# Roll along rows: half rows of two neighbours per DMA in place of one whole row

## The chip, the cores and the metric

The kernel runs on one core of one Trainium2 chip. The metric is the device time of one execution in microseconds. Data moves through 16 DMA engines that serve several queues; the queues that matter here are filled by SyncE (SP), ScalarE (ACT) and GpSimd (POOL).

## The reference

```python
def reference(x, shift):              # x: 8192 x 8192 float32, shift = 100
    return np.roll(x, shift, axis=1)
```

Every row is moved right by 100 elements (400 bytes), and its last 100 elements become its first. There is no arithmetic: 268.44 MB are read and 268.44 MB written.

## The kernel before

Each row of 8192 elements (32 KB) is cut at column `a` of the output. With `s = 100`, line 20 gives 128 and line 22 raises it to `a = 256`; `g = a - s = 156`.

**Bodies.** Columns `a` to 8192 of the output (7936 elements, 31744 bytes a row) are copied straight from HBM to HBM, from columns 156 to 8092 of the input. The rows are seen as 128 blocks of 64, and a block as 16 groups `e` of four neighbouring rows `j` (lines 34 and 35). One DMA at line 44 takes row `j` of each of the 16 groups: the trace gives it 16 pieces of 31744 bytes. Its 16 rows stand four rows (128 KB) apart, one for each DMA engine, so an engine gets four neighbouring rows one after another from four DMAs. SP starts at block 0 and goes up, with `j` rising; ACT starts at block 127 and goes down, with `j` falling (line 42). The two loops run in step for `i` from 0 to 63. For the last two values of `i` each row is issued as two DMAs of one half each, cut at `mid = 4224`: `parts` in line 40.

No body depends on another. On each of the two queues the semaphores that the framework gives out turn in fours, so from the fifth DMA on an issue waits until the DMA four before it has landed.

**Heads.** Columns 0 to 255 of the output go through on-chip tiles on GpSimd's queue: 16 tiles of 512 rows, four rows to each of 128 partitions. Line 73 loads, in runs of 1024 bytes, the last 100 elements of one row together with the first 156 of the next, for three of the four rows; lines 74 and 77 load what is missing at the ends; VectorE puts the pieces into place (lines 75 and 78), and line 81 writes 256 columns of all 512 rows. All tiles have buffers of their own.

Of the kernel before, what the change touches and what calls it, by code (L numbers as in the profile page):

```python
# [1 line left out]

# [4 lines left out]


@with_exitstack
def kernel(  # L10
    ctx: ExitStack,
    tc: tile.TileContext,
    x: bass.AP,
    shift: int,
    out: bass.AP,
):
    nc = tc.nc
    n_rows, n_cols = x.shape
    s = shift % n_cols
    a = -(-s // 128) * 128  # L20
    if 0 < a <= 384 and a + 128 <= n_cols:
        a += 128
    g = a - s
    P = nc.NUM_PARTITIONS
    engines = [nc.sync, nc.scalar]
    n_chunks = 16
    rows = n_rows // n_chunks

    xm = x.rearrange("(c e j) w -> c j e w", e=16, j=4)
    om = out.rearrange("(c e j) w -> c j e w", e=16, j=4)
    if a < n_cols:
        blocks = n_rows // 64
        mid = (a + n_cols) // 256 * 128
        for i in range(blocks // 2):
            parts = ((a, mid), (mid, n_cols)) if i >= blocks // 2 - 2 and a < mid else ((a, n_cols),)  # L40
            for j in range(4):
                for eng, c, q in ((engines[0], i, j), (engines[1], blocks - 1 - i, 3 - j)):
                    for lo, hi in parts:
                        eng.dma_start(out=om[c, q, :, lo:hi], in_=xm[c, q, :, lo - s:hi - s])
    if a == 0:
        return


    if a > 512:
        for i in range(n_chunks):  # L50
            r = slice(i * rows, (i + 1) * rows)
            nc.gpsimd.dma_start(out=out[r, :s], in_=x[r, n_cols - s:])
            if g > 0:
                nc.gpsimd.dma_start(out=out[r, s:a], in_=x[r, :g])
        return

    Q = 4
    n_st = n_rows // (P * Q)
    reads = ctx.enter_context(tc.tile_pool(name="reads", bufs=n_st))
    heads = ctx.enter_context(tc.tile_pool(name="heads", bufs=n_st))
    xt = x.rearrange("(k p q) c -> k p q c", q=Q, p=P)
    ot = out.rearrange("(k p q) c -> k p q c", q=Q, p=P)
    tiles = []
    for k in range(n_st):
        t = reads.tile([P, Q - 1, a], x.dtype)
        h = heads.tile([P, Q, a], x.dtype)  # L70
        lead = bass.AP(tensor=x.tensor, offset=(k * P * Q + 1) * n_cols - s,
                       ap=[[Q * n_cols, P], [n_cols, Q - 1], [1, a]])
        nc.gpsimd.dma_start(out=t[:], in_=lead, single_packet=True)  # L73
        nc.gpsimd.dma_start(out=h[:, Q - 1, :s], in_=xt[k, :, Q - 1, n_cols - s:], single_packet=True)  # L74
        nc.vector.tensor_copy(h[:, :Q - 1, :s], t[:, :, :s])  # L75
        if g > 0:
            nc.gpsimd.dma_start(out=h[:, 0, s:], in_=xt[k, :, 0, :g], single_packet=True)  # L77
            nc.vector.tensor_copy(h[:, 1:, s:], t[:, :, s:])  # L78
        tiles.append(h)
    for k, h in enumerate(tiles):  # L80
        nc.gpsimd.dma_start(out=ot[k, :, :, :a], in_=h[:], single_packet=True)  # L81


# [1 line left out]
_INS = ['x', 'shift']  # L85
_OUTS = [((8192, 8192), 'float32')]

_NUMBERS = {'shift': 100}


# [26 lines left out]
```

## Time and profile before

| what | value |
|---|---|
| median of 3 runs | 816.4 us (815.55 to 817.09) |
| the profiled execution | 817.74 us, of which 816.0 us is the span of the profile |
| GpSimd busy | 41.3 us in 68 instructions |
| VectorE busy | 12.0 us in 32 instructions |
| issues of whole-row DMAs | 248 on SP, 248 on ACT, 496 KB each |
| issues of half-row DMAs (the last two `i`) | 16 on SP, 16 on ACT, 248 KB each |
| issues for the heads | 64 on GpSimd's queue |

The span runs from the first to the last recorded work; the profiled execution's own time contains it. "DMA" rows give the busy share of the 16 DMA engines in tenths for 40 equal slices, and GB/s what they moved (each byte once, though an HBM to HBM copy both reads and writes it). In the list of queues, q1 is SP's, q10 is ACT's and q0 is GpSimd's; the columns are packets, MB, and the time that the packets took as a share of 16 engines' span. The packet records hold queue, size, start and duration of each packet, but not the number of its engine. In the list of DMA issues the columns are KB of each and median us from issue to landing.

### The profile page before, as it was taken

The page shows a single profiled execution, that of the slowest core. Times are in us where ns is not written, and L with a number is a line of the kernel's source. Part 1 is how long each engine was busy: PE and PEld are TensorE (multiplying, and loading weights), DVE is VectorE, ACT ScalarE, POOL GpSimd, SP SyncE. Part 2 cuts the span into 40 slices and gives each one's busy share as a digit, 9 for nine tenths or more (in the row PEclk, how much of TensorE's full clock was granted, in tenths as well). Part 3 has the DMA queues.
Part 4 walks back from the last instruction along what each step waited for, and adds up shares of the span by engine and source line. Part 5 has one row for each costly group of instructions (what it writes and reads, how often), then busy time and mean ns, then how long its engine had stood idle before and what let it go on. Part 6 is the DMA issues. An engine that isn't in the chain of part 4 may idle for free. (4 is left out here: it accounts for less than half of the span.)

```text
span 816.0 us, 689 instructions
## 1 busy us (share of the span) xinstructions
DVE 12.0 (1%) x32; POOL 41.3 (5%) x68
## 2 busy tenths in 40 slices
DVE  0000000000000000000000000000000000000000
POOL 2001011101110110000000000000000000000000
DMA  9999999999999999999999999999999999999998
GB/s 315 348 338 362 340 353 342 355 336 347 338 355 348 350 365 354 353 352 347 352 355 344 328 336 324 335 333 336 333 332 336 333 327 341 328 332 333 339 302 297
DMA packets 22277, 276.90 MB, mean 339 GB/s; under 512 B 9472, under 2 KB 9728, under 8 KB 13824
## 3 DMA queue, kind: packets, MB, share of 16 engines
q1 hardware_dynamic: 8448, 130.04, 46.6%
q10 hardware_dynamic: 8448, 130.04, 43.7%
q0 software_dynamic: 5376, 16.78, 8.6%
q14 instruction: 5, 0.04, 0.0%
HBM read 268.44 MB, written 268.44 MB: 658 GB/s over the span
## 5 line engine op out<-in xcount | busy, mean ns | idle before, releaser
L81 POOL DMA_DIRECT2D out_dram<-h x16 | 11.4, 715 | 146.7 <-DMA out_dram<-h 91.7
L77 POOL DMA_DIRECT2D h<-in_x_dram x16 | 8.7, 542 | 156.0 <-DMA t<-in_x_dram 156.0
L73 POOL DMA_DIRECT2D t<-in_x_dram x16 | 12.2, 762 | 23.6 <-DMA h<-in_x_dram 22.8
L74 POOL DMA_DIRECT2D h<-in_x_dram x16 | 8.9, 559 | 37.2 <-DMA h<-in_x_dram 37.2
L75 DVE COPY h<-t 128x300 f32<-128x300 f32 x16 | 5.9, 367 | 271.5 <-DMA t<-in_x_dram 271.5
L78 DVE COPY h<-t 128x468 f32<-128x468 f32 x16 | 7.5, 468 | 0.0
L98 POOL MEMSET const-float32-0.0<- 128x1 f32 x1 | 0.1, 99 | 0.2 <-issue 0.2
L98 POOL MEMSET const-bfloat16-1.0<- 128x1 bf16 x1 | 0.1, 102 | 0.0
L98 POOL MEMSET const-float32-1.0<- 128x1 f32 x1 | 0.1, 99 | 0.0
L98 POOL MEMSET const-uint8-127<- 128x1 uint8 x1 | 0.1, 99 | 0.0
## 6 DMA issues: line engine op xcount, KB each, us to landing
out_dram<-in_x_dram SPq DMA_DIRECT2D x248, 496.0 KB, 12.7
out_dram<-in_x_dram ACTq DMA_DIRECT2D x248, 496.0 KB, 12.7
out_dram<-h POOLq DMA_DIRECT2D x16, 512.0 KB, 105.6
t<-in_x_dram POOLq DMA_DIRECT2D x16, 384.0 KB, 47.8
out_dram<-in_x_dram SPq DMA_DIRECT2D x16, 248.0 KB, 6.0
out_dram<-in_x_dram ACTq DMA_DIRECT2D x16, 248.0 KB, 5.9
h<-in_x_dram POOLq DMA_DIRECT2D x16, 78.0 KB, 41.6
h<-in_x_dram POOLq DMA_DIRECT2D x16, 50.0 KB, 47.5
```

What stands on the lines that cost most here:

```text
L73: nc.gpsimd.dma_start(out=t[:], in_=lead, single_packet=True)
L74: nc.gpsimd.dma_start(out=h[:, Q - 1, :s], in_=xt[k, :, Q - 1, n_cols - s:], single_packet=True)
L75: nc.vector.tensor_copy(h[:, :Q - 1, :s], t[:, :, :s])
L77: nc.gpsimd.dma_start(out=h[:, 0, s:], in_=xt[k, :, 0, :g], single_packet=True)
L78: nc.vector.tensor_copy(h[:, 1:, s:], t[:, :, s:])
L81: nc.gpsimd.dma_start(out=ot[k, :, :, :a], in_=h[:], single_packet=True)
L98: nc = _bacc.Bacc("TRN2", target_bir_lowering=False, num_devices=1)
```

## The change

For `i` from 0 to 61 the four DMAs of a block are cut the other way. Where a DMA took row `j` whole for each of the 16 groups, it now takes one half (columns 256 to 4223, or 4224 to 8191, 15872 bytes each) of two neighbouring rows of each group. The order on SP in a block is: left halves of rows 0 and 1, right halves of rows 0 and 1, left halves of rows 2 and 3, right halves of rows 2 and 3. ACT takes rows 2 and 3 first and then 0 and 1, also left halves before right. The `rearrange` puts `e` outermost, so the 16 groups still go to the 16 engines. Bytes and issues stay as they were. The last two values of `i` and the heads are untouched.

```diff
         for i in range(blocks // 2):
             parts = ((a, mid), (mid, n_cols)) if i >= blocks // 2 - 2 and a < mid else ((a, n_cols),)
+            if len(parts) == 1 and a < mid:
+                for j in (0, 2):
+                    for lo, hi in ((a, mid), (mid, n_cols)):
+                        for eng, c, q in ((engines[0], i, j), (engines[1], blocks - 1 - i, 2 - j)):
+                            eng.dma_start(out=om[c, q:q + 2, :, lo:hi].rearrange("j e w -> e j w"),
+                                          in_=xm[c, q:q + 2, :, lo - s:hi - s].rearrange("j e w -> e j w"))
+                continue
             for j in range(4):
                 for eng, c, q in ((engines[0], i, j), (engines[1], blocks - 1 - i, 3 - j)):
                     for lo, hi in parts:
```

## The prediction

> **What bounds the kernel now.** I read the DMA rows first, because sections 1 and 5 of the page hold only 12.0 us of VectorE and 41.3 us of GpSimd work in a span of 816.0 us. From the page:
>
> ```profile
> DMA  9999999999999999999999999999999999999998
> DMA packets 22277, 276.90 MB, mean 339 GB/s; under 512 B 9472, under 2 KB 9728, under 8 KB 13824
> q1 hardware_dynamic: 8448, 130.04, 46.6%
> q10 hardware_dynamic: 8448, 130.04, 43.7%
> q0 software_dynamic: 5376, 16.78, 8.6%
> HBM read 268.44 MB, written 268.44 MB: 658 GB/s over the span
> ```
>
> The 16 DMA engines are busy from end to end: 46.6 + 43.7 + 8.6 = 98.9%. q1 (SP) and q10 (ACT) carry the row bodies, HBM to HBM; q0 (GpSimd) carries 16.78 MB of row heads through the on-chip tiles. Busy is not full speed, though. In the packet records, 31744 B (one row body) takes 1173 ns at best, 1430 ns on average (1475 on q1, 1384 on q10); only a third are under 1185 ns. So engines mostly hold a packet longer than they need to move it. What holds them shows in the same window view, first with GpSimd's queue running and then with the copies alone:
>
> ```profile
> 20.00:490.00 470.00, 11.94 (x32) 35.95 (x56) 1.00 1.00 347
> 490.00:760.00 270.00, 0.00 (x0) 0.00 (x0) 1.00 0.99 333
> ```
>
> The last column is GB/s moved, the one before it the DMA share. A copied byte is both read from and written to HBM; a GpSimd byte touches HBM once. The DMA view of the first stretch has 16.23 MB on q0, 34.5 GB/s over 470 us. HBM traffic is therefore 2 x 347 - 34.5 = 659.5 GB/s in the first and 2 x 333 = 666 in the second: two mixtures that differ by 14 GB/s in bytes moved agree within 1% in HBM traffic. I read the bound as the memory's throughput under this pattern, about 660 GB/s, and not the number of packets.
>
> Then the issuers, in the waits of SP's queue and the DMA issues:
>
> ```profile
> SPq L44 <- DMA out_dram<-in_x_dram: 670.1, 258, 5.1
> out_dram<-in_x_dram SPq DMA_DIRECT2D x248, 496.0 KB, 12.7
> out_dram<-in_x_dram SPq DMA_DIRECT2D x16, 248.0 KB, 6.0
> ```
>
> SP sits waiting 670.1 us: the trace's semaphores on this queue turn in fours, so an issue waits for the DMA four before it. Four DMAs in flight on each queue, 12.7 us from issue to landing, is a full backlog; issue time (510 ns on SP, 517 on ACT) is off the path.
>
> **The change, part by part.** Per block of 64 rows each queue still issues four DMAs of 496 KB in place of four of 496 KB, for all but the last two values of i. So the 248 + 248 whole-row DMAs, their semaphores, their waits and their bytes stay; each of the 16 engines now gets two pieces of 15872 B where it got one of 31744 B.
>
> Packets: 496 DMAs x 16 engines = 7936 pieces become 15872, 496 more per engine. Undisturbed, the trace has 1175 ns (median of the quick ones) for a whole row and 592 ns (median on q1 and q10) for a half, which the last 32 DMAs already carry: 2 x 592 - 1175 = 9 ns per split, 496 x 9 ns = 4.5 us if every one showed. Two thirds of the packets are held longer than they need anyway and hide it; a third run at full speed. I take 4.5 / 3 = 1.5 us, with 0 (all covered by memory stalls) and 4.5 us (none covered) as ends.
>
> The Trainium skill, page "DMA: Bandwidth & Descriptors", section "How a descriptor splits into AXI transactions", says a descriptor that doesn't start on a multiple of 256 B reads from the boundary below it and discards what lies before. The new right halves start in the source at byte 4124 x 4 = 16496, 112 past such a boundary, so by that page (an estimate) 7936 x 112 B = 0.9 MB more would be read, 1.3 us at 660 GB/s; no row of this trace can show it.
>
> Order: an engine takes one packet from q1, then one from q10 (chained by end and start, 1401 of the 1712 row packets of q10 between 420 and 750 us follow a q1 row directly). With half pieces I expect the turns to come at half rows, so four address streams (two reads, two writes) alternate twice as often, and each 32 KB row is visited in two visits with its neighbour's half between. Traffic under finer mixing is what this trace shows least. The nearest rows are the two stretches: with GpSimd's pieces of 400 to 4096 B in the turn, traffic is 1% lower (659.5 against 666), which over the kernel would be 8 us. On the other side stands the best 20 us slice of the copy-only part, 341 GB/s against 333, worth 2.3% or 19 us less if it held throughout; the worst there is 322 to 324, 3% or 25 us more. The last 32 DMAs say that half rows by themselves are harmless: mean packet 708 ns against 1430 / 2 = 715, landing 6.0 against 12.7 / 2 = 6.35 us, though those run as the backlog drains. I take 2 us, a quarter of the 8: pieces of 15872 B are far longer than GpSimd's.
>
> Completion: an SP DMA now ends after ACT's first half too, about one half piece (0.7 us) later in its turn. That shifts SP's next issue once and is hidden by three more DMAs queued behind; if that cover were gone, engines would idle, where they now have a share of 0.99. What SP and ACT queue behind the wait is only more copies, so nobody else is late.
>
> GpSimd: its packets stand in the same turns. If turns halve, its loads land sooner (now 47.8 us for 384 KB) and its last issue comes well before 404 us. That moves when its 16.78 MB go, not how many bytes the memory carries: cost 0. The drain after 780 us keeps its DMAs unchanged.
>
> Sum: 1.5 + 2 = 3.5 us. On the profiled execution (817.74 us, of which 816.0 is span) that is 821.2; the median of the runs is 816.4, 1.3 below that execution, so 820 us.
>
> **The rivals.** *Hidden altogether* (816.4, within 0.2%): the splits vanish in memory stalls and order makes no difference; the steady 660 GB/s speaks for it. The change may also not interleave at all: if an engine takes both pieces of a DMA in one turn, only the 9 ns splits are left, at most 4.5 us.
>
> *Faster*: the pattern, not the bytes, sets the 660 GB/s. Whole-row turns let one stream hold an engine for up to 3.3 us (longest row packet); shorter turns even out the engines and spread the accesses. Place: the copies throughout; price: half of the way from 333 to 341 GB/s, 1.2% or 10 us, 806 us. It decides once the copy-only stretch rises above about 335 GB/s. For it: the spread of packet times, and a rate that wanders from 322 to 341 with nothing else changed. Against it: two different mixtures reach the same traffic, as a ceiling would have it.
>
> *Much slower*: the 16 engines work on rows 128 KB apart (four rows of 32 KB), now all in the same half of their rows for a whole DMA; if that crowds fewer parts of memory, the rate falls to the worst slices, 323 GB/s, 3%: 841 us. Against it: whole rows also start together and keep 333 to 347. [...]
>
> **How the numbers follow.** A measurement of this kernel can tell about 0.2% (1.6 us) from no change. Forecast, a small loss of 818 to 824 us: 0.38. Much slower, 824 to 845: 0.17. Hidden: 0.14. Faster: 0.31, most of it between 803 and 814. So slower 0.55, same 0.14, faster 0.31. The range 803 to 836 leaves out the last fifth of the way from 816.4 to the 841 of the worst slices and the gains beyond 1.6%, about one case in ten. Both signs hold much of the chance; the forecast's own range is 818 to 824.
>
> **What would show it.** Unchanged: 248 + 248 issues of 496 KB, DMA share 9 throughout, 510 ns issues. Packets rise by 7936 to about 30200. The copy-only stretch should fall from 333 to about 331 or 332 GB/s, and section 3 should show q1 and q10 a little busier for the same 130.04 MB. If turns halve, GpSimd's loads land clearly below 47.8 us and its last L81 issue comes before 404 us. I am wrong if the copy-only rate is at 335 or above (memory liked the order) or below 325 (it disliked it), or if engine share falls under 0.97 (issue became the bound).

## The result: 819.1 against 816.8 us, and the profile after

The changed kernel takes 819.08 us (median of 15 runs), the kernel before 816.81 us (15 runs beside it): ratio 1.0027, 95% interval 1.0018 to 1.0035, so 2.3 us slower (1.5 to 2.9). The profiled execution takes 819.45 us, 817.7 of it span. Its page, with the rows in the order shown of before:

```profile
DMA  8999999999999999999999999999999999999998
DMA packets 30213, 276.90 MB, mean 339 GB/s; under 512 B 9472, under 2 KB 9728, under 8 KB 13824
q1 hardware_dynamic: 12416, 130.04, 47.1%
q10 hardware_dynamic: 12416, 130.04, 43.9%
q0 software_dynamic: 5376, 16.78, 8.0%
HBM read 268.44 MB, written 268.44 MB: 657 GB/s over the span
```

7936 packets more (30213 - 22277), the same bytes, engines still busy throughout, and 657 in place of 658 GB/s of HBM traffic. Against before, q1 is up 0.5 and q10 0.2 points of engine time and q0 is down 0.6. The same stretches as before:

```profile
20.00:490.00 470.00, 11.27 (x30) 34.57 (x54) 1.00 1.00 348
490.00:760.00 270.00, 0.00 (x0) 0.00 (x0) 1.00 0.99 332
```

The copies alone run at 332 GB/s where they ran at 333: 0.3% as rounded, 0.2% by the packet records (663.3 against 664.7 GB/s of HBM traffic). The 348 against 347 of the first stretch is no gain: GpSimd's packets are now gone by 378 us (507 us before), and the copies that fill the rest of the stretch move fewer bytes a second; the HBM traffic of that stretch is 660.4 GB/s in both. Summed over the packet records, the new kernel's HBM traffic is behind by 0.7 us at 20 us, 0.8 at 350, 1.6 at 440, 0.5 at 500, 1.3 at 750 and 1.7 at 805 (bytes missing at 663 GB/s). The gap wanders by about 1 us, so one pair of profiles can't tell where in the run the 1.7 us between the two spans are lost. The issues:

```profile
SPq L45 <- DMA out_dram<-in_x_dram: 636.4, 244, 5.0
out_dram<-in_x_dram SPq DMA_DIRECT2D x248, 496.0 KB, 12.6
t<-in_x_dram POOLq DMA_DIRECT2D x16, 384.0 KB, 37.4
L45 SPq DMA_DIRECT2D out_dram<-in_x_dram x248: 571/571/717, 0.7 to 782.8; - x124
```

The last line (durations in ns, least/median/most, then the first and last start in us) shows an issue at 571 ns where a whole row's took 510; with 636 us of waiting in front of them the issues hide that. GpSimd's loads land in 37.4 in place of 47.8 us, and its last write is issued at 298 us in place of 404.

### The profile page after: what moved, and what is told of

Same layout as the page of the kernel before. It is cut to its first block, busy times and chain, and to the rows that moved or that the text cites. A ratio compares the mean times of both kernels' runs of the same rounds, so it can differ in the third digit from the quotient of the medians.

```text
span 817.7 us, 689 instructions
## 1 busy us (share of the span) xinstructions
DVE 12.0 (1%) x32; POOL 41.2 (5%) x68
## 2 busy tenths in 40 slices
DMA packets 30213, 276.90 MB, mean 339 GB/s; under 512 B 9472, under 2 KB 9728, under 8 KB 13824
## 5 line engine op out<-in xcount | busy, mean ns | idle before, releaser
L80 POOL DMA_DIRECT2D t<-in_x_dram x16 | 12.2, 760 | 13.6 <-DMA h<-in_x_dram 12.7
## 6 DMA issues: line engine op xcount, KB each, us to landing
t<-in_x_dram POOLq DMA_DIRECT2D x16, 384.0 KB, 37.4
```

## The experiments

They ran in three later jobs, each on another chip, where the kernel before took 826.9, 829.9 and 829.1 us, so ratios to it are compared; where two profiles of different jobs are set side by side, the text says so. The first job held the change once more, the half pieces in old order, the crossed pairs and the quarters; the third held the eighths, with and without heads and at both shifts, and the two rows per DMA; the second held the rest. In the code, "..." and comments stand for lines left out, and a line with "-" is what the new one takes the place of; the last two values of `i` stay as they were.

**Theories.** *Split*: the loss is the number of pieces, a fixed cost for each. *Order*: it is the row left half way. My prediction had both, 1.5 and 2 us. A rival for the cause is that finer turns let GpSimd's small packets in more often.

**The change once more**, to compare with the other kernels of the first of these jobs:

> The change itself, beside the others on one chip: 1.0027 within 1.0018 to 1.0035.

Measured: 1.0027 (1.0016 to 1.0038).

**Half pieces, old order.** Each engine walks its rows from start to end as before, but a DMA carries the right half of one row and the left half of the next:

```diff
-eng.dma_start(out=om[c, q, :, a:n_cols], in_=xm[c, q, :, a - s:n_cols - s])
+...                                    # half DMAs at the two ends of each queue
+row = (c * 64 + q) * n_cols
+# nxt: next row of this engine on this queue (j + 1, or the next block's first)
+ap = [[4 * n_cols, 16], [nxt + a - row - mid, 2], [1, mid - a]]
+eng.dma_start(out=bass.AP(tensor=out.tensor, offset=row + mid, ap=ap),
+              in_=bass.AP(tensor=x.tensor, offset=row + mid - s, ap=ap))
```

> Half-row pieces in the order of before: a DMA carries the right half of one row and the left half of the next, so each engine walks its rows from start to end as before, but in pieces of 15872 B with two per DMA (one extra half DMA at each end of each queue). Theory 1, the split: the loss comes from the number of pieces (9 ns each, partly covered) and from turns at half rows, so this kernel loses the same, ratio to before about 1.003 (819 us). Theory 2, the order: the loss comes from leaving a row half way and coming back to it, so this kernel is at 1.000 (817 us). Both at once, as predicted (1.5 us for the split, 2 us for the order): 1.001 to 1.002. If the pieces stand in finer turns, GpSimd's loads land in about 37 us as after the change, in every theory.

Measured: 1.0024 (1.0012 to 1.0037). That is the change's loss without the change's order. What is left for the order is 0.03%, some 0.2 us, with about 1.4 us either way. GpSimd's loads land in 35.1 us, near the 37 expected, so turns are finer here too. One side effect: a DMA that runs from the end of one row to the start of the next has the head columns between its two pieces, and the framework makes the heads' writes wait for bodies. The waits of this kernel show it; before, the longest wait of that line was for earlier writes of heads, 91.7 us in total:

```profile
POOL out_dram L96 <- DMA out_dram<-in_x_dram: 612.0, 15, 91.2
```

The heads' writes are spread over the whole run there (the last q0 packet ends at 810 us), and yet the time is that of the changed kernel. So where the heads' bytes fall in time seems to cost nothing, unless it happens to offset the order; no run has one without the other.

**Crossed pairs.** A DMA carries the left half of one row and the right half of its neighbour, the next DMA the two others (set against the changed kernel):

```diff
-    for lo, hi in ((a, mid), (mid, n_cols)):
+    for first, step in ((a, n_cols + w), (mid, n_cols - w)):      # w = mid - a
...
+            ap = [[4 * n_cols, 16], [step, 2], [1, w]]
```

> The same pieces and DMAs as after the change, other pairs: a DMA carries the left half of one row and the right half of the next, the following DMA the two halves left over. Theory 1 (the split): as after the change, 1.003. Theory 2 (the order): the row is left half way as often as after the change, so also about 1.003, but if it matters whether the pieces of a DMA lie in the same half of the row (all engines in one half, the rival of crowding), it falls back to 1.000 to 1.001.

Measured: 1.010 (1.0062 to 1.0139), and this takes in only the three quickest of its six runs (830.6, 836.7 and 839.1 us); the others took 863.4 to 897.3, and the profiled one is the longest, with a span of 895.5. It does not answer its question, since the pattern brought waits of its own: the instructions rise from 689 to 937, 244 of the 248 more are semaphore instructions of SP and ACT, and SP's longest wait grows from 5.1 to 9.4 us. The framework evidently takes DMAs to overlap that share no element. Here and in the half pieces of the old order the two pieces of a DMA lie in different rows and in different columns of them; the change and the eighths, whose DMAs take the same columns of every row and span each other's columns as well, have the 689 instructions of before. From 200 to 760 us:

```profile
200.00:760.00 560.00, 0.00 (x0) 7.15 (x10) 1.00 0.88 301
```

Engine share 0.88 and 301 GB/s: here engines run out of work. It is a picture of the case that the prediction named as its third alarm (share under 0.97), by waits and not by issue time, and the change itself avoids it.

**More splits.** Quarters of four rows per DMA, then eighths (each DMA: two eighths of four rows), bytes and number of DMAs kept:

```diff
-parts = ((a, mid), (mid, n_cols)) ... else ((a, n_cols),)          # before: whole rows
+for lo in range(a, n_cols, w):                                     # w = (n_cols - a) // 4
+    for eng, c in ((engines[0], i), (engines[1], blocks - 1 - i)):
+        eng.dma_start(out=om[c, :, :, lo:lo + w].rearrange("j e w -> e j w"),
+                      in_=xm[c, :, :, lo - s:lo - s + w].rearrange("j e w -> e j w"))
```
```diff
+ap = [[4 * n_cols, 16], [n_cols, 4], [4 * w, 2], [1, w]]           # w = (n_cols - a) // 8
+for lo in range(a, mid, w): ...
```

Quarters:

> The change carried one step on: a DMA carries one quarter (7936 B) of four neighbouring rows per engine, so 23808 splits in place of 7936 and turns at quarter rows. Theory 1 (the split): three times the splits, so three times the loss, about 1.008 (823 us); with the stalls covering a rising share, at least 1.005. Theory 2 (the order): each row is visited four times in place of two, three returns in place of one: also up to 1.008, but as the pieces shrink it may fall either way. A ceiling of the memory that nothing of this touches: 1.003 again. GpSimd's loads should land sooner still, about 30 us, if turns are taken at each piece.

Eighths:

> Eighth pieces (3968 B): a DMA carries the eighths n and n + 4 of four neighbouring rows per engine, 55552 splits, same bytes and number of DMAs. With 4.6 ns of an engine per split, as halves and quarters gave: 16 us, ratio 1.019. If the heads' packets are what finer turns disturb, the loss flattens (the heads can't get sooner than at full turns): 1.012.

Measured: quarters 1.0084 (1.0066 to 1.0102), eighths 1.0190 (1.0165 to 1.0214). GpSimd's loads land in 24.6 us with quarters and 14.9 with eighths. With 7936, 23808 and 55552 splits the losses are 0.27, 0.84 and 1.90%: 0.27 to 0.28% for each 7936 splits. That is a straight line through nothing, as a fixed price would have it: 15.8 us over 3472 splits per engine is 4.5 ns for one, halves (2.2 us over 496) give 4.5 and quarters 4.7. But the line alone doesn't prove a fixed price, since more than the number of splits differs: all halves and quarters start 112 B past a multiple of 256 B in the source, while every second eighth starts 240 B past one there and 128 B past one in the output (3968 is 15.5 times 256); and whether order costs anything was tried for halves only. The loss shows in the copy-only stretch of the eighths, where the half rows had 328 GB/s in the first of these jobs. q1 and q10 together hold 93.7% of the engines' time, 91.3% there, but part of that is time that GpSimd's queue no longer holds (5.9 in place of 8.2%):

```profile
490.00:760.00 270.00, 0.00 (x0) 0.00 (x0) 1.00 1.00 319
q1 hardware_dynamic: 36224, 130.04, 49.7%
q10 hardware_dynamic: 36224, 130.04, 44.0%
```

**Without heads.** Columns 0 to 255 are not written:

```diff
-    if a == 0:
+    if a > 0:
         return
```

> The kernel before without the heads (columns 0 to 255 of the output are not written). A ceiling of the memory at about 660 GB/s: 16.78 MB of 536.9 MB less HBM traffic, 3.1% less time, ratio 0.969. A bound by the DMA engines' own time: the share of GpSimd's queue, 8.6%, falls away, ratio 0.914.

> Quarter pieces without the heads (columns 0 to 255 are not written), to set beside the bodies of before without heads. If a split costs about 4.5 ns of an engine wherever it stands, this is 0.8% above that kernel. If the loss came from GpSimd's packets getting more turns, the two are the same within 0.2%.

> Eighth pieces without the heads (columns 0 to 255 are not written), against the bodies of before without heads, 0.9656. Cost of a split independent of the heads: the same 16 us, 0.985. Quarters lost 0.34% without heads and 0.84% with them; if that holds on, 7/3 of 0.34% here: 0.8%, ratio 0.973.

Measured: before without heads 0.9656 (0.9644 to 0.9669). That is near the 0.969 of a ceiling on HBM traffic and far from the 0.914 of a bound by engine time. The window from 20 to 760 us of that kernel, then of the quarters and of the eighths without heads:

```profile
20.00:760.00 740.00, 0.00 (x0) 1.00 1.00 327
```
```profile
20.00:760.00 740.00, 0.00 (x0) 1.00 1.00 325
```
```profile
20.00:760.00 740.00, 0.00 (x0) 1.00 1.00 323
```

Engine share stays at 1.00 with a queue's 8.6% gone: the copies' packets are held longer (31744 B now 1538 ns on average over both queues). Busy engines here are waiting engines. By the packet records this kernel moves 655 GB/s of HBM traffic from 20 to 760 us; in the same job whole rows with heads, at a shift of 128, move 654. So reads and writes of HBM together are what is level; whether the memory itself or the way to it sets that level, no run here tells. Quarters are at 0.9689 and eighths at 0.9821, so against the bodies alone the loss is 0.34% (about 0.18 either way) and 1.71% (0.22, across two jobs). Eighths lose nearly what they lost with heads (1.90%), so most of the price of a split is the bodies' own. Quarters lose less than half of their 0.84% in time, though the two profiles, 327 and 325 GB/s, lie 0.6% apart; why quarters and eighths don't agree is open.

**Starts at multiples of 256 B.** With a shift of 128 the output is rolled by 128, and whole rows, halves and quarters start at a multiple of 256 B in the source as they already did in the output. For the eighths this holds of every second piece only: the others go from 240 B past a multiple to 128 B past one, in the source, and stay 128 B past one in the output, so that what was expected of them as fully aligned doesn't apply. Either way each start comes 112 B nearer to the multiple below it:

```diff
-_NUMBERS = {'shift': 100}
+_NUMBERS = {'shift': 128}
```

Whole rows:

> The kernel before with a shift of 128 elements in place of 100 (the result is rolled by 128), so that each piece starts at a multiple of 256 B in the source too. Same bytes, same pieces. If the memory reads in whole blocks of 256 B from the boundary below, 7936 starts of 112 B less are 0.9 MB or 0.2%: ratio 0.998. If not: 1.000.

Quarters:

> Quarter pieces with a shift of 128 (the result is rolled by 128). With a shift of 100 quarters cost 0.84% over whole rows. If the cost of a split is the engine's or the turn's, it stays: 0.8% above the kernel before with a shift of 128. If it is the bytes read below an unaligned start (112 B x 23808 = 2.7 MB, 4 us at 650 GB/s), 4 us of the 6.9 us vanish: 0.3 to 0.4% above it.

Eighths:

> Eighth pieces with a shift of 128 (the result is rolled by 128), so that every piece starts at a multiple of 256 B in the source; to be set against the kernel before with that shift, 0.9973. Bytes read below unaligned starts as the cause: 112 B x 55552 = 6.2 MB, 9.5 us at 655 GB/s, vanish, so about 0.8% above it (1.005). Engine time per split as the cause: the same distance as with a shift of 100, 1.016 or more.

Measured: 0.9973 (0.9961 to 0.9984), 1.0031 (1.0018 to 1.0044) and 1.0087 (1.0069 to 1.0106). Against whole rows of the same shift, quarters cost 0.58% (0.17 either way) and eighths 1.14% (0.22, across two jobs), where they cost 0.84 and 1.90% at shift 100. For quarters the difference, 0.26%, is no larger than its uncertainty; for eighths 0.76% (0.33), 6.3 us, goes away. So the price of a split has two parts. About 1.8 of the eighths' 4.5 ns go with the shift. Of the quarters' 4.7 ns, 3.2 (about 0.9 either way) stay with every start aligned; the 2.7 ns that stay for the eighths still hold their unaligned half. The quick packets don't show the difference: a quarter takes 300 ns and an eighth 154 (medians) at either shift. A shift of 128 also changes the distance between source and output addresses and the length of the heads' pieces, so the first part is tied to the shift, not proven to be extra bytes read. The copies alone at shift 128, eighths from 490 to 760 us (319 at shift 100):

```profile
490.00:760.00 270.00, 0.00 (x0) 0.00 (x0) 1.00 1.01 324
```

**The other way: two whole rows per DMA.**

```diff
-for j in range(4): ... om[c, q, :, a:n_cols]
+for j in (0, 2): ... om[c, q:q + 2, :, a:n_cols].rearrange("j e w -> e j w")
```

> The other direction: a DMA carries two whole neighbouring rows per engine (992 KB), no split, half the DMAs and half the 4-byte completion packets, twice the bytes in flight. If the number of packets costs time, 248 fewer completion packets per engine and queue at 9 ns, half of it shown: 0.2% less, 0.998. If the memory alone decides: 1.000. Neither expects a loss, unless the deeper queues disturb the heads or the end.

Measured: 1.0132 (1.0111 to 1.0153). A loss, which neither theory expected. Pieces are as before, half the DMAs, twice the bytes in flight (the completion packets saved are 124 per engine and queue, 8448 - 6464 packets on q1 over 16 engines, not 248). The issues and the last 36 us:

```profile
out_dram<-in_x_dram SPq DMA_DIRECT2D x124, 992.0 KB, 26.0
out_dram<-h POOLq DMA_DIRECT2D x16, 512.0 KB, 153.6
```
```profile
800.00:836.00 36.00, 0.00 (x0) 0.00 (x0) 1.00 0.79 273
```

Against the profile of the change in the first of these jobs (both from the packet records), 4.6 MB more HBM traffic is left at 760 us, 7 us at its rate, and what is left then moves at 601 in place of 637 GB/s, 4 us more. The kernel before took 2.2 us longer in the job of the two rows, so about that much of the 11 us is not theirs. The second part is the drain: engine share 0.79, probably as some engines run out before others. Why the traffic is lower ahead of it, with share 1.00, wasn't tried; landing times of 26.0 in place of 12.7 us leave the engines free to drift twice as far apart, which may be it.

## Why the prediction was right, and which terms were not

- **The bound.** Right as a level of HBM traffic, and shown: taking the heads away saved 3.4%, close to their 3.1% of the HBM traffic and not their 8.6% of the engines' time. That the memory itself sets the level is the prediction's reading.
- **The split term, 1.5 us.** Too small, within its ends of 0 and 4.5. Measured: 2.0 us by the half pieces in old order (0.24%). The 9 ns per split of the undisturbed packets was the right quantity (quarters: 4 x 300 - 1175 = 25 ns for 3 splits, 8.3 each; eighths: 8 x 154 - 1175 = 57 ns for 7, 8.1 each); the share that shows was a half, 4.5 ns, and not the third of packets that ran at full speed. With aligned starts (quarters) it is 3.2 ns, about that third. The page "DMA: Bandwidth & Descriptors" of the Trainium skill (section "How a descriptor splits into AXI transactions") has the bytes below an unaligned start read and dropped. By an estimate from that rule (112 B fewer below each of 55552 starts) the shift of 128 should have won back 9.5 us for the eighths; 6.3 us (about 2.7 either way) came back. The direction agrees, the size is just outside the interval, and the sum had left this out. The halves were not run at that shift, so how much of the change's own 2.3 us goes with the starts stays open.
- **The order term, 2 us.** Not borne out: 0.2 us, with about 1.4 either way, so 2 us lies outside. It was read from a stretch with GpSimd's small pieces in the turn, a row that has nothing of this order in it. The two errors lie in opposite directions; that is why 3.5 us stood near the measured 2.3, and so far the closeness is luck.
- **Turns at half rows.** Only in part in the profile of the change: chained by end and start with gaps of up to 4 ns either way, about 73% of q10's row pieces between 420 and 750 us follow a piece of q1 directly and about 25% another of q10 (before, 1669 of 1712, 97%, follow one of q1; the prediction's 1401 took in fewer). So about half of the time an engine still took both pieces of a DMA in a row. When the change was run once more, about nine in ten pieces followed one of q1, and the loss was 0.27% again. GpSimd's loads gained as forecast in kind, 47.8 to 37.4 us.
- **Hidden things.** GpSimd's earlier end cost nothing that these runs can tell, as forecast; the later completions of SP neither (share 0.99 to 1.00). "510 ns issues unchanged" was wrong, 571 ns, with no effect.
- **Copy-only rate.** 332 of the forecast 331 or 332 GB/s.
- **The rivals.** Faster would have needed 335 GB/s. Crowding into one half of the rows would have shown as a loss that the old order doesn't have; the half pieces in the old order lose the same within 1.4 us.

What stays open: whether the 3 ns that stay at a shift of 128 are the packet's handling itself or the finer turns that come with it, since no kernel here splits without changing the turns (the two profiles of the change, with unlike turns and like losses, speak for the handling, but they are one execution each); what in the shift saves the rest; and the quarters without heads.

## What to carry to other kernels

When the engines show 99% busy, ask whether they move bytes or hold them: compare the best packet with the mean one, and count HBM traffic (a copied byte twice, a loaded one once) over stretches with different mixtures. If it is level, expect little from a rearrangement that keeps bytes and backlog: splitting rows won nothing here and cost 0.24 to 1.90%, because a price per piece still shows in part. Test such a small effect by multiplying it (three and seven times the splits), which turned 0.27% into a line that could be read, and check that nothing else grows with it, as the unaligned starts of the eighths do here.

## What the runs showed of the hardware

- A split cost 4.5 to 4.7 ns of an engine at a shift of 100, half of its undisturbed 8 to 9 ns, over three sizes of piece (15872, 7936 and 3968 B), while whole rows, one per DMA, kept reads and writes together at 654 to 665 GB/s. With every start at a multiple of 256 B, quarters cost 3.2 ns a split (about 0.9 either way).
- Twice the bytes in flight with the same pieces, in half as many DMAs, cost 1.3%.
- The shift by 128 in place of 100 elements made the whole-row kernel 0.27% faster (0.16 to 0.39).
- Of the framework: DMAs whose two pieces lie in different rows and different columns of them brought waits though no element is shared: 248 more instructions in the crossed pairs, with an engine share of 0.88 in the longest run, and 612 us of waiting heads' writes in the half pieces of the old order, which cost no time.
